# Routing two token blocks at a time, and all operand splits of an output phase on VectorE

## The chip, the cores and the metric

One core of one Trainium2 chip runs the whole program. The metric is the device time of one launch in microseconds (us). TensorE (PE) does the matrix products, VectorE (DVE), ScalarE (ACT) and GpSimd (POOL) the elementwise work; each engine runs its own queue of instructions in order, and SyncE (SP) issues most of the transfers. PEld is TensorE loading its weights, which goes on beside the products.

## What is computed

One decoder layer on 1024 tokens of width 1024: a norm and an input projection, two groups of causal attention heads, a norm for each group, an output projection, then a router and experts, and at the end a gated embedding and a norm. The change concerns the part from the output projection to the router:

```python
x = x + jnp.concatenate([o_sb, o_df], axis=-1) @ w_out
h2 = _rmsnorm(x, g_ffn).reshape(-1, D_MODEL)
group_logits = h2 @ w_router_group + b_router_group
g_idx = jnp.argmax(group_logits, axis=-1)
g_w = softmax(group_logits)[g_idx]
in_group = (h2 @ w_router_expert + b_router_expert)[group g_idx]
top_vals, top_idx = lax.top_k(in_group, 2)
top_w = softmax(top_vals) * g_w
for e in range(16):
    y = y + gates[:, e] * (silu(h2 @ w_gate[e]) * (h2 @ w_up[e])) @ w_down[e]
```

Each token goes to two of 16 experts. The kernel computes only these two: it numbers the tokens of each expert (their rank), keeps the lists of token numbers in `slots`, and later fetches the rows of an expert by an indirect transfer.

## The kernel before

The tokens are handled in eight blocks of 128. To keep accuracy every large operand is **split** into a rounded high part and a remainder: `split` (L53) rounds on ScalarE (L54) and subtracts on VectorE, or on the engine that is handed in (L55). A product then takes three matrix instructions, high by high, high by low, and low by high (L1162 to L1164).

Attention runs until about 590 us, its last part beside the first blocks of the output phase. The class `OutPhase` does for each block b: `normed(b)` (L1124), which loads the attention output, scales it (L1136, L1141) and splits it, on GpSimd for b of 2 and more (L1144); `proj_items(b)` (L1147), two halves of 24 products each with an addition on VectorE (L1166); `tail(b)` (L1201), which transposes the sum (L1194), splits the transposed tile from the accumulator memory (PSUM) (L1195), multiplies by the router's weights (L1210) and norms the block (L116); and `routes(b)`, the call of `route` (L1287), a chain of some 33 short instructions on VectorE. The chain takes the maximum of the group logits (L1298), marks the winner (`pick`, L1275), masks the other groups (L1308), picks the first and second expert (L1311 to L1316), adds both marks to `A` (L1325), has TensorE count ranks (L1327, L1328), builds two rows of marks (L1336), has TensorE put the token numbers in their places (L1343), and adds these to `slots` (L1345). `items(b)` (L1172) puts `normed(b + 1)` beside the second step of block b, and `tail(b - 1)` and `routes(b - 1)` among its later steps; the tail and the routing of the last block come after all of it.

Beside blocks 3 to 7 the weights of the first expert are loaded and split ahead: `moe.start` (L1667) splits three tiles on GpSimd, and at block 5 `moe.weights(1, nc.gpsimd)` two more (L1041). After the last routing `route_tail` (L1350) turns `slots` into lists of indices, while TensorE computes five blocks of the embedding's product (`ple_back`, L1465); then the rows of the first expert are fetched (L1507), transposed (L1516), and the experts' loop begins (L1681).

Outside the stretches marked as a manual schedule a planner orders each engine's queue before the program runs. It works with its own estimate of every instruction's length, and among instructions that it holds to be ready it takes the one that stands earlier in the program. On the chip the order is fixed: an engine stands before an instruction whose operands are late, even if a later one could go.

Of the kernel before, what the change touches and what calls it, by code (L numbers as in the profile page):

```python
# [25 lines left out]
CAP = 192  # L26
# [9 lines left out]
def bcast(ap, n):  # L36
    return bass.AP(tensor=ap.tensor, offset=ap.offset, ap=[[0, 128], [1, n]])
# [728 lines left out]
def run_items(*streams):  # L766

    tot = [sum(c for c, _ in s) or 1.0 for s in streams]
    pos = [0] * len(streams)
    done = [0.0] * len(streams)  # L770
    while True:
        live = [i for i in range(len(streams)) if pos[i] < len(streams[i])]
        if not live:
            return
        i = min(live, key=lambda x: (done[x] + 0.5 * streams[x][pos[x]][0]) / tot[x])
        c, f = streams[i][pos[i]]
        f()
        done[i] += c
        pos[i] += 1
# [36 lines left out]
def first_pair(k, P, pa, pp):  # L816
# [37 lines left out]
    def norm(b, parts=1):  # L854
        return normed(k, b, r[b], g, parts)
# [95 lines left out]
def phase_attention(k, moe, pq):  # L951
    nc, tc = k.nc, k.tc
# [12 lines left out]
    start = ExitStack()  # L965
# [101 lines left out]
class OutPhase:  # L1067
# [56 lines left out]
    def normed(self, b):  # L1124
        k, nc, wk = self.k, self.k.nc, self.wk
        if b % 2 == 0:
            self.scales(b // 2)
        rs = self.rs[b // 2]
        cols = lambda t: t.rearrange("p (c q) -> p c q", c=NC)
        raw = cols(self.oraw[b % 2])  # L1130
        nc.sync.dma_start(raw, k.oT_d[:, :, b * 128:(b + 1) * 128].rearrange("c p s -> p c s"))
        sc = lambda i: rs[:, b % 2, i:i + 1].to_broadcast([128, 128])
        bc = self.bank("t")
        nc.tensor.transpose(bc[:, 0:128], sc(0), k.ident)
        for c in range(4):
            nc.vector.scalar_tensor_tensor(raw[:, c, :], raw[:, c, :], self.gn[:, c:c + 1], bc[:, 0:128],  # L1136
                                           op0=OP.mult, op1=OP.mult)
        bc = self.bank("t")
        for i in range(4):
            nc.tensor.transpose(bc[:, i * 128:(i + 1) * 128], sc(1 + i), k.ident)  # L1140
        nc.vector.scalar_tensor_tensor(raw[:, 4:8, :], raw[:, 4:8, :], self.gn[:, 4:5],  # L1141
                                       bc.rearrange("p (c q) -> p c q", c=4), op0=OP.mult, op1=OP.mult)
        oh, ol = cols(self.onh[b % 2]), cols(self.onl[b % 2])
        split(nc, oh, ol, raw, nc.gpsimd if b > 1 else nc.vector)  # L1144
        self.O[b] = oh, ol

    def proj_items(self, b):  # L1147
# [74 lines left out]
        self.lg[b] = lg, r  # L1222

    def routes(self, b):
        route(self.k, b, *self.lg.pop(b))


def route_consts(k):
    nc = k.nc
    p = k.cp  # L1230
# [41 lines left out]
    nc.vector.memset(k.slots, 0.0)  # L1272


def pick(k, sc, m, n, wts):  # L1275

    nc, rt = k.nc, k.rt
    v = rt.tile([128, n], FT, name="pk_v", bufs=3)
    vm = rt.tile([128, 1], FT, name="pk_m", bufs=6)
    oh = rt.tile([128, n], FT, name="pk_o", bufs=6)  # L1280
# [3 lines left out]
    return oh, vm  # L1284


def route(k, b, lg, rstd):  # L1287
    nc, rt = k.nc, k.rt
    col = lambda nm: rt.tile([128, 1], FT, name=nm, bufs=2)
    L = rt.tile([128, 20], FT, name="L")  # L1290
    tp = k.bank("t")[:, 0:80]
    for x in range(2):
        nc.tensor.transpose(tp[:, 40 * x:40 * x + 40], lg[:, 128 * x:128 * x + 128], k.ident[0:40, 0:40])
    nc.vector.reduce_sum(L, tp.rearrange("p (x n) -> p n x", x=4), axis=AX)
    nc.vector.scalar_tensor_tensor(L, L, rstd, k.br, op0=OP.mult, op1=OP.add)
    G, E = L[:, 0:4], L[:, 4:20]
# [3 lines left out]
    eg = rt.tile([128, 4], FT, name="eg")  # L1300
    nc.scalar.activation(eg, G, AF.Exp, bias=ng, accum_out=sg)
    gw = col("gw")
    nc.vector.reciprocal(gw, sg)
    og, _ = pick(k, G, gm, 4, k.wt16[:, 12:16])
    pen = rt.tile([128, 4], FT, name="pen")
    nc.vector.tensor_scalar(pen, og, 1.0, 1e30, op0=OP.subtract, op1=OP.mult)
    Lm = rt.tile([128, 16], FT, name="Lm")
    nc.vector.tensor_tensor(Lm.rearrange("p (g e) -> p g e", g=4), E.rearrange("p (g e) -> p g e", g=4),  # L1308
                            pen[:, :, None].to_broadcast([128, 4, 4]), OP.add)
    m1, m2 = col("m1"), col("m2")  # L1310
    nc.vector.reduce_max(m1, Lm, axis=AX)  # L1311
    o1, _ = pick(k, Lm, m1, 16, k.wt16)
    L2 = rt.tile([128, 16], FT, name="L2")
    nc.vector.scalar_tensor_tensor(L2, o1, -3e30, Lm, op0=OP.mult, op1=OP.add)
    nc.vector.reduce_max(m2, L2, axis=AX)
    o2, _ = pick(k, L2, m2, 16, k.wt16)  # L1316
    d, e21, den = col("dd"), col("e21"), col("den")
    nc.vector.tensor_tensor(d, m2, m1, OP.subtract)
    nc.scalar.activation(e21, d, AF.Exp)
    nc.vector.tensor_scalar(den, e21, 1.0, None, op0=OP.add)  # L1320
    nc.vector.reciprocal(den, den)
    nc.vector.tensor_tensor(k.wts[:, 0, b:b + 1], den, gw, OP.mult)
    nc.vector.tensor_tensor(k.wts[:, 1, b:b + 1], k.wts[:, 0, b:b + 1], e21, OP.mult)
    A = rt.tile([128, 16], BF, name="A")
    nc.vector.tensor_tensor(A, o1, o2, OP.add)  # L1325
    rk = k.bank("sm")
    nc.tensor.matmul(rk[:, 0:16], k.tri, A, start=True, stop=False)  # L1327
    nc.tensor.matmul(rk[:, 0:16], k.onesb, k.acum, start=False, stop=True)  # L1328
    nc.vector.tensor_tensor(k.acum, k.acum, A, OP.add)
    put = []  # L1330
    for i, o in enumerate((o1, o2)):
        j16 = rt.tile([128, 16], FT, name="j16")
        r = k.rank[:, i, b:b + 1]
        nc.vector.scalar_tensor_tensor(j16, rk[:, 0:16], 1.0, o, op0=OP.mult, op1=OP.mult, accum_out=r)
        row = rt.tile([128, CAP], BF, name="row", bufs=2)
        nc.vector.tensor_scalar(row, k.ios, r, None, op0=OP.is_equal)  # L1336
        ids = rt.tile([128, 2, 16], BF, name="ids", bufs=2)
        nc.vector.tensor_tensor(ids, o[:, None, :].to_broadcast([128, 2, 16]),
                                k.tok[:, i, b, :, None].to_broadcast([128, 2, 16]), OP.mult)
        put.append((row, ids))  # L1340
    for rows, lo, n, x in (((0, 128), 0, 128, 32), ((0, 64), 128, 64, 64), ((64, 128), 128, 64, 64)):
        for i, (row, ids) in enumerate(put):
            nc.tensor.matmul(rk[rows[0]:rows[1], x:x + 32], row[:, lo:lo + n], ids.rearrange("p a e -> p (a e)"),  # L1343
                             start=(i == 0), stop=(i == 1))
    nc.vector.tensor_tensor(k.slots, k.slots, rk[:, 32:96].rearrange("p (s a e) -> p s a e", s=2, a=2), OP.add)  # L1345
    for i, o in enumerate((o1, o2)):
        nc.gpsimd.tensor_copy(k.chose[:, i, b, :], o)


def route_tail(k, rt):  # L1350
# [139 lines left out]
class Moe:  # L1490
# [513 lines left out]
```

## Time and profile before

| what | us |
|---|---|
| median of 3 runs (range) | 1231.78 (1230.64 to 1232.29) |
| the profiled execution, its own time | 1227.81 |
| its span, first to last instruction | 1226.0 |
| TensorE busy in it | 1145.5 (93%) |
| VectorE busy | 923.1 (75%) |
| ScalarE busy | 723.0 (59%) |
| GpSimd busy | 207.5 (17%) |
| mean granted TensorE clock | 0.979 of full speed |

Shares of the whole span mix stages with different limits. The stage of the change lies between about 500 and 702 us of the span, so that is where the rows of the prediction are read. An idle time of TensorE that stands in brackets behind a row of the timeline names what ended it.

### The profile page before, as it was taken

The numbers are of one execution on the slowest core, as the hardware profiler recorded it, in microseconds if no ns is written. First come the engines' busy times: TensorE is split into PE (matmuls) and PEld (weight loads), VectorE is DVE, ScalarE is ACT, GpSimd is POOL, SyncE is SP. The second block draws the span as 40 slices with busy tenths as digits, with TensorE's granted clock in tenths as the row PEclk, the third lists the DMA queues.
The fourth block names the chain that finished last, engine by engine and source line by source line (L and its number), as shares of the span: only waits on it lengthen the run. The fifth ranks groups of instructions, "written<-read, shape, count | busy, mean of one in ns | idle before, by whom it ended". The sixth has DMA issues, their size and how long they took to land. (4 is left out here: it accounts for less than half of the span.)

```text
span 1226.0 us, 22814 instructions
## 1 busy us (share of the span) xinstructions
PE 1145.5 (93%) x8181; PEld 826.5 (67%) x8181; DVE 923.1 (75%) x2144; ACT 723.0 (59%) x1408; POOL 207.5 (17%) x298
## 2 busy tenths in 40 slices
PE   5999999999999999889789899999999999997996
PEld 4766656665666666646444498898998989883443
DVE  7677786766766767769888777777888878765875
ACT  6476766766756576735332365666777767663432
POOL 0133333333200000002331101111112212110000
PEclk9999999999999999879899999999999999999999
DMA  6212021120222121532674878998998999937611
GB/s 208 67 30 74 30 69 32 44 60 27 57 61 65 40 65 53 171 90 102 217 234 148 298 250 262 282 352 265 316 313 283 337 280 325 304 125 298 250 71 52
DMA packets 211756, 202.54 MB, mean 165 GB/s; under 512 B 12697, under 2 KB 182681, under 8 KB 211642
## 3 DMA queue, kind: packets, MB, share of 16 engines
q1 hardware_dynamic: 205688, 180.22, 46.9%
q0 software_dynamic: 5808, 20.58, 4.5%
q8 instruction: 65, 1.06, 0.3%
q14 instruction: 49, 0.40, 0.1%
q10 hardware_dynamic: 146, 0.27, 0.1%
HBM read 163.03 MB, written 29.62 MB: 157 GB/s over the span
## 5 line engine op out<-in xcount | busy, mean ns | idle before, releaser
L228 PE MATMUL mm<-hT,whi 128*128 128x512 f32 (+1 forms) x416 | 210.9, 508 | 2.6 <-DVE rs_v L66 1.4
L229 PE MATMUL mm<-hT,whi 128*128 128x512 bf16 (+1 forms) x416 | 157.0, 377 | 4.1 <-DVE hT L184 4.1
L230 PE MATMUL mm<-hT,wlo 128*128 128x512 bf16 (+1 forms) x416 | 155.7, 374 | 0.0
L1611 PE MATMUL gu<-xh,mhiu 128*128 128x128 f32 (+4 forms) x512 | 155.1, 314 | 0.0
L1611 PE MATMUL gu<-xh,mhig 128*128 128x128 f32 (+4 forms) x512 | 153.9, 308 | 0.0
L1613 PE MATMUL gu<-xbl,mhig 128*128 128x128 bf16 (+4 forms) x512 | 124.6, 243 | 2.6 <-DVE xbl L1524 2.6
L1613 PE MATMUL gu<-xbl,mhiu 128*128 128x128 bf16 (+4 forms) x512 | 124.4, 243 | 0.0
L1614 PE MATMUL gu<-xh,mblg 128*128 128x128 bf16 (+4 forms) x512 | 119.6, 234 | 0.0
L1614 PE MATMUL gu<-xh,mblu 128*128 128x128 bf16 (+4 forms) x512 | 119.3, 233 | 0.0
L55 DVE TENSOR_TENSOR mdl<-mrawd,mdh 128x1024 bf16<-128x1024 f32 x63 | 77.0, 1222 | 44.6 <-ACT mdh L54 39.9
L54 ACT ACTIVATE wth<-tp 128x512 fp32r<-128x512 f32 (+2 forms) x168 | 70.2, 446 | 63.0 <-PE tp L378 41.0
L55 DVE TENSOR_TENSOR wtl<-tp,wth 128x512 fp32r<-128x512 f32 (+2 forms) x168 | 79.2, 493 | 36.7 <-ACT wth L54 35.3
L409 POOL TENSOR_TENSOR row<-row,keep 128x127 f32<-128x127 f32 (+3 forms) x64 | 77.9, 1218 | 143.5 <-DVE keep L408 88.4
L228 PEld LDWEIGHTS mm<-hT,whi 128*128 128x128 f32 x416 | 80.2, 193 | 30.9 <-ACT hT L183 2.0
L55 DVE TENSOR_TENSOR mblg<-mrawg,mhig 128x1024 bf16<-128x1024 f32 x62 | 75.8, 1223 | 29.8 <-ACT mhig L54 29.7
L54 ACT ACTIVATE mdh<-mrawd 128x1024 fp32r<-128x1024 f32 x64 | 67.6, 1056 | 51.8 <-PE ya L1643 47.6
L1611 PEld LDWEIGHTS gu<-xh,mhig 128*128 128x128 f32 x512 | 97.6, 191 | 0.7 <-ACT xh L1523 0.3
L229 PEld LDWEIGHTS <-whi 128*128 128x128 bf16 x416 | 40.7, 98 | 85.0 <-issue 78.6
L1611 PEld LDWEIGHTS gu<-xh,mhiu 128*128 128x128 f32 x512 | 96.7, 189 | 0.0
L408 DVE TENSOR_TENSOR_SCAN keep<-keep,zx 128x128 f32<-128x128 f32 (+3 forms) x64 | 85.4, 1346 | 14.1 <-ACT keep L404 13.4
L46 POOL DMA_INDIRECT y_d<-yo,put x27 | 44.6, 1651 | 290.0 <-ACT yo L1661 185.8
L54 ACT ACTIVATE mhig<-mrawg 128x1024 fp32r<-128x1024 f32 x64 | 67.4, 1053 | 19.2 <-PE gu L1614 11.9
(348 smaller groups left out, 3346.6 us busy)
## 6 DMA issues: line engine op xcount, KB each, us to landing
mrawg<-in_w_expert_gate_dram SPq DMA_DIRECT2D x64, 512.0 KB, 5.8
mrawu<-in_w_expert_up_dram SPq DMA_DIRECT2D x64, 512.0 KB, 6.4
mrawd<-in_w_expert_down_dram SPq DMA_DIRECT2D x64, 512.0 KB, 4.3
wraw<-in_w_in_dram SPq DMA_DIRECT2D x24, 512.0 KB, 3.9
yg<-y_d SPq DMA_DIRECT2D x16, 512.0 KB, 5.7
xt<-in_x_dram SPq DMA_DIRECT2D x8, 512.0 KB, 6.6
oT_d<-ot SPq DMA_DIRECT2D x32, 128.0 KB, 2.1
wraw<-in_w_out_dram SPq DMA_DIRECT2D x8, 512.0 KB, 3.6
```

What stands on the lines that cost most here:

```text
L46: i = k.nc.gpsimd.indirect_dma_start(out=out, out_offset=bass.IndirectOffsetOnAxis(ap=idx, axis=0), in_=src, in_offset=None)
L54: nc.scalar.activation(hi, src, AF.Copy)
L55: (eng or nc.vector).tensor_tensor(lo, src, hi.bitcast(FT), OP.subtract)
L228: nc.tensor.matmul(ps, hi[:, c, :], hT[:, c % 4, :], start=(c == 0), stop=False)
L229: nc.tensor.matmul(ps, wv[:, c, :], k.hT[half][2][:, c, o:o + n], start=False, stop=False)
L230: nc.tensor.matmul(ps, lo[:, c, :], hv[:, c % 4, :], start=False, stop=(c == NC - 1))
L408: nc.vector.tensor_tensor_scan(a, a, k.zeros.to_broadcast([128, n]), 1.0, op0=OP.mult, op1=OP.add)
L409: nc.gpsimd.tensor_tensor(beta[:, :n - 1], beta[:, :n - 1], keep[:, 1:n], OP.mult)
L1611: nc.tensor.matmul(ps[:, x], hi[:, c], xh[:, c], start=(c == 0), stop=False)
L1613: nc.tensor.matmul(ps[:, x], hv[:, c], xl[:, c], start=False, stop=False)
L1614: nc.tensor.matmul(ps[:, x], bl[:, c], xv[:, c], start=False, stop=(c == NC - 1))
```

## The change

The routing is cut in two. `logits` makes the 20 logits of one block and leaves them in half of a shared tile `k.L`; it runs where `route` ran. `route` now runs after each odd block only, on both blocks at once: its small tiles get a dimension of two. As the maximum that `pick` compares with is no longer one value per partition, its first instruction (compare and multiply) becomes two. The ranks of the second block are counted with one more product, which adds the first block's `A`. The four rows of marks are built one after the other, their twelve products go to separate places of one PSUM bank, and one reduction adds them up before `slots` is updated. The weights of the two experts (`k.wts`) and the copy to `chose` on GpSimd come last, once for both blocks.

All five weight tiles split ahead, and the attention output of blocks 2 to 7, are split on VectorE. GpSimd keeps the copies to `chose`, the memsets and the indirect transfers.

```diff
-            moe.weights(1, nc.gpsimd)
+            moe.weights(1)
...
-        split(nc, oh, ol, raw, nc.gpsimd if b > 1 else nc.vector)
+        split(nc, oh, ol, raw)
...
     def routes(self, b):
-        route(self.k, b, *self.lg.pop(b))
+
+        logits(self.k, b, *self.lg.pop(b))
+        if b % 2:
+            route(self.k, b - 1)
...
-    nc.vector.scalar_tensor_tensor(v, sc, m, wts, op0=OP.is_equal, op1=OP.mult)
+    nc.vector.tensor_tensor(v, sc, over(m), OP.is_equal)
+    nc.vector.tensor_tensor(v, v, wts[:, None, :].to_broadcast([128, 2, n]), OP.mult)
     nc.vector.reduce_max(vm, v, axis=AX)
-    nc.vector.tensor_scalar(oh, v, vm, None, op0=OP.is_equal)
...
+    nc.vector.tensor_tensor(oh, v, over(vm), OP.is_equal)
...
+    A = one("A", 16, BF)
+    nc.vector.tensor_tensor(A, O[:, 0], O[:, 1], OP.add)
+    rk = k.bank("sm")
+    for y in range(2):
+        r = rk[:, 16 * y:16 * y + 16]
+        nc.tensor.matmul(r, k.tri, A[:, y], start=True, stop=False)
+        if y:
+            nc.tensor.matmul(r, k.onesb, A[:, 0], start=False, stop=False)
+        nc.tensor.matmul(r, k.onesb, k.acum, start=False, stop=True)
+    nc.vector.tensor_tensor(k.j16, rk[:, 0:32].rearrange("p (y e) -> p y e", y=2)[:, None].to_broadcast([128, 2, 2, 16]),
+                            O, OP.mult)
+    nc.vector.reduce_sum(k.rank[:, :, two], k.j16, axis=AX)
+    for i in range(2):
+        nc.vector.tensor_tensor(k.ids[:, i], O[:, i, :, None, :].to_broadcast([128, 2, 2, 16]),
+                                k.tok[:, i, two, :, None].to_broadcast([128, 2, 2, 16]), OP.mult)
+    for i in range(2):
+        for y in range(2):
+            row = rt.tile([128, CAP], BF, name="row", bufs=2)
+            nc.vector.tensor_scalar(row, k.ios, k.rank[:, i, b + y:b + y + 1], None, op0=OP.is_equal)
+            ids = k.ids[:, i, y].rearrange("p a e -> p (a e)")
+            for rows, lo, n, x in (((0, 128), 0, 128, 32), ((0, 64), 128, 64, 64), ((64, 128), 128, 64, 64)):
+                x += 64 * (2 * i + y)
+                nc.tensor.matmul(rk[rows[0]:rows[1], x:x + 32], row[:, lo:lo + n], ids, start=True, stop=True)
+    new = k.j16.rearrange("p i y e -> p (i y e)")
+    nc.vector.reduce_sum(new, rk[:, 32:288].rearrange("p (z n) -> p n z", z=4), axis=AX)
+    nc.vector.tensor_tensor(k.slots, k.slots, new.rearrange("p (s a e) -> p s a e", s=2, a=2), OP.add)
+    for y in range(2):
+        nc.vector.tensor_tensor(k.acum, k.acum, A[:, y], OP.add)
...
     def start(self):
         self.wp = self.pool("mw", 2)
-        self.weights(0, self.k.nc.gpsimd)
-        self.weights_down(0, self.k.nc.gpsimd)
+        self.weights(0)
+        self.weights_down(0)
```

## Rows read from the trace of the kernel before

**Rows 1.** Busy time of each engine in a stretch of 20 us: stretch, its length, then PE, PEld, DVE, ACT and POOL busy with their instructions, granted TensorE clock, share of the DMA engines, GB/s.

```profile
580.00:600.00 20.00, 17.16 (x103) 10.31 (x101) 18.03 (x66) 9.12 (x18) 9.12 (x8) 1.00 0.80 270
```

**Rows 2.** Timeline of TensorE: start, length, instruction, and in brackets the idle time before it and what ended it.

```profile
577.36 0.66 PE L378 MATMUL tp<-ident,row 128*128 128x128 f32 x4 [0.79 <-DVE wtl L55]
...
603.91 1.07 PE L1210 MATMUL dsm<-od,wr 128*40 128x256 f32 x4 [6.74 <-DVE od L55]
...
619.32 0.19 PE L1343 MATMUL dsm<-ids,row 128*128 128x32 bf16 x1 [1.28 <-DVE row L1336]
...
633.00 0.17 PE L1327 MATMUL dsm<-A,tri 128*128 128x16 bf16 x1 [2.10 <-DVE A L1325]
...
653.80 0.17 PE L1327 MATMUL dsm<-A,tri 128*128 128x16 bf16 x1 [2.06 <-DVE A L1325]
...
663.95 0.18 PE L1327 MATMUL dsm<-A,tri 128*128 128x16 bf16 x1 [0.28 <-DVE A L1325]
```

**Rows 3.** The same columns as in rows 1, in stretches of 4 us around two of those idle times.

```profile
604.00:608.00 4.00, 4.00 (x15) 2.35 (x16) 0.56 (x3) 0.38 (x1) 0.00 (x0) 0.50 1.03 312
608.00:612.00 4.00, 4.00 (x16) 1.68 (x15) 3.58 (x16) 2.28 (x4) 1.05 (x1) 0.87 0.11 31
...
632.00:636.00 4.00, 3.00 (x15) 1.55 (x14) 2.75 (x26) 0.20 (x1) 0.20 (x1) 0.62 1.06 275
```

**Rows 4.** The splits on GpSimd: all of them by the tile that they write (lengths in ns, lowest/median/highest, then first and last start).

```profile
L55 POOL TENSOR_TENSOR od<-od,od x6: 2358/2388/2878, 554.4 to 650.6; 128x1024 bf16<-128x1024 f32 x6
L55 POOL TENSOR_TENSOR mblg<-mrawg,mhig x2: 2371/2380/2388, 591.0 to 615.7; 128x1024 bf16<-128x1024 f32 x2
L55 POOL TENSOR_TENSOR mblu<-mrawu,mhiu x2: 2378/2380/2381, 593.7 to 622.4; 128x1024 bf16<-128x1024 f32 x2
L55 POOL TENSOR_TENSOR mdl<-mrawd,mdh x1: 2336/2336/2336, 598.7 to 598.7; 128x1024 bf16<-128x1024 f32 x1
```

**Rows 5.** Timeline of VectorE: instructions that began beside a split on GpSimd, one of the same kind with no such split beside it (590.96), and the two splits of a transposed block that TensorE waited for (603.17).

```profile
573.29 2.35 DVE L80 TENSOR_SCALAR rs_y<-rs_i 128x1 int32<-128x1 int32 x2
...
590.96 0.17 DVE L71 TENSOR_TENSOR rs_t<-rs_t,rs_v 128x10 f32<-128x10 f32 x1
591.07 2.31 DVE L75 SCALAR_TENSOR_TENSOR rs_t<-rs_y,rs_v 128x1 f32<-128x1 f32 x1
...
594.99 1.13 DVE L84 TENSOR_SCALAR rs_t<-rs_t 128x1 f32<-128x1 f32 x2
...
596.38 2.34 DVE L71 TENSOR_TENSOR rs_t<-rs_y 128x10 f32<-128x10 f32 x1
...
598.75 2.26 DVE L71 TENSOR_TENSOR rs_t<-rs_t,rs_v 128x10 f32<-128x10 f32 x1
...
603.17 1.28 DVE L55 TENSOR_TENSOR od<-dt,od 128x512 fp32r<-128x512 f32 x2
...
615.79 2.35 DVE L1323 TENSOR_TENSOR wts<-wts,e 128x1 f32<-128x1 f32 x1
...
622.64 2.14 DVE L71 TENSOR_TENSOR rs_y<-rs_y,rs_t 128x1 f32<-128x1 f32 x1
...
650.62 2.35 DVE L1281 SCALAR_TENSOR_TENSOR pk_v<-L,m,wt 128x16 f32<-128x16 f32 x1
```

**Rows 6.** A split of the same shape on VectorE, two of them as a group of the stretch from 540 to 690 us: busy time, mean ns of one, idle before.

```profile
L55 DVE TENSOR_TENSOR pll<-mrawd,plh 128x1024 bf16<-128x1024 f32 x2 | 2.4, 1214 | 0.0
```

**Rows 7.** Timeline of VectorE: the routing of block 5 (its second instruction, the rows of marks, the last), the addition of a projection within it, and a reduction of 256 elements elsewhere.

```profile
659.27 0.24 DVE L1295 SCALAR_TENSOR_TENSOR L<-L,rs_y,br 128x20 f32<-128x20 f32 x1
...
662.58 0.68 DVE L1166 TENSOR_TENSOR od<-mm,od 128x512 f32<-128x512 f32 x1
...
664.49 0.45 DVE L1336 TENSOR_SCALAR row<-ios,rank 128x192 bf16<-128x192 bf16 x2
...
665.40 0.22 DVE L1345 TENSOR_TENSOR slots<-slots,dsm 128x64 f32<-128x64 f32 x1
...
692.40 0.41 DVE L1377 TENSOR_REDUCE cn_place<-cn_m 128x16 f32<-128x256 f32 x1
```

**Rows 8.** The end of the phase, from the timelines of three engines: the last instruction of the last projection, the last routing's second and last instruction, the second fetch, the last product of the embedding, and the first transpose for the experts.

```profile
677.10 0.39 PE L1164 MATMUL mm<-woh,od 128*128 128x512 bf16 x1
...
697.09 0.39 PE L1476 MATMUL pq<-plh,pTl 128*128 128x512 bf16 x1
699.18 0.71 PE L1516 MATMUL mt<-ident,xr 64*128 64x64 f32 x8 [1.71 <-DMA xr<-h_d,idx]
...
683.74 0.23 DVE L1295 SCALAR_TENSOR_TENSOR L<-L,rs_y,br 128x20 f32<-128x20 f32 x1
...
690.42 0.22 DVE L1345 TENSOR_TENSOR slots<-slots,dsm 128x64 f32<-128x64 f32 x1 [0.67 <-PE dsm L1343]
...
693.61 0.91 POOL L1507 DMA_INDIRECT xr<-h_d,idx  x1 [0.30 <-PE pq L1476]
```

**Rows 9.** What TensorE waited for from 702 us to the end, the largest: total us, times, longest.

```profile
PE pq L1459 <- issue: 4.9, 1, 4.9
```

**Rows 10.** Timeline of ScalarE, the high parts of two of the weight tiles; and from the page's costliest groups the experts' own splits on VectorE (busy, mean ns, idle before and what ended most of it).

```profile
592.58 1.06 ACT L54 ACTIVATE mhiu<-mrawu 128x1024 fp32r<-128x1024 f32 x1 [1.69 <-DMA mrawu<-in_w_expert_up_dram]
...
621.24 1.06 ACT L54 ACTIVATE mhiu<-mrawu 128x1024 fp32r<-128x1024 f32 x1
...
L55 DVE TENSOR_TENSOR mblg<-mrawg,mhig 128x1024 bf16<-128x1024 f32 x62 | 75.8, 1223 | 29.8 <-ACT mhig L54 29.7
```

More of the change, by code (lines that the diff above doesn't have):

```diff
@@ L1272, in route_consts, with pick, logits @@
     nc.vector.memset(k.slots, 0.0)
-def pick(k, sc, m, n, wts):
+def pick(k, sc, m, n, wts, oh):
     nc, rt = k.nc, k.rt
-    v = rt.tile([128, n], FT, name="pk_v", bufs=3)
-    vm = rt.tile([128, 1], FT, name="pk_m", bufs=6)
-    oh = rt.tile([128, n], FT, name="pk_o", bufs=6)
-    nc.vector.scalar_tensor_tensor(v, sc, m, wts, op0=OP.is_equal, op1=OP.mult)
-    nc.vector.reduce_max(vm, v, axis=AX)
-    nc.vector.tensor_scalar(oh, v, vm, None, op0=OP.is_equal)
[L1284 to L1290, printed above, removed]
+    over = lambda x: x[:, :, None].to_broadcast([128, 2, n])
+    v = rt.tile([128, 2, n], FT, name="pk_v", bufs=2)
+    vm = rt.tile([128, 2], FT, name="pk_m", bufs=3)
+    nc.vector.tensor_tensor(v, sc, over(m), OP.is_equal)
+    nc.vector.tensor_tensor(v, v, wts[:, None, :].to_broadcast([128, 2, n]), OP.mult)
+    nc.vector.reduce_max(vm, v, axis=AX)
+    nc.vector.tensor_tensor(oh, v, over(vm), OP.is_equal)
+def logits(k, b, lg, rstd):
+    nc = k.nc
     tp = k.bank("t")[:, 0:80]
@@ L1293, in route @@
         nc.tensor.transpose(tp[:, 40 * x:40 * x + 40], lg[:, 128 * x:128 * x + 128], k.ident[0:40, 0:40])
+    L = k.L[:, b % 2, :]
     nc.vector.reduce_sum(L, tp.rearrange("p (x n) -> p n x", x=4), axis=AX)
     nc.vector.scalar_tensor_tensor(L, L, rstd, k.br, op0=OP.mult, op1=OP.add)
-    G, E = L[:, 0:4], L[:, 4:20]
+def route(k, b):
+    nc, rt = k.nc, k.rt
+    two = slice(b, b + 2)
+    col = lambda nm: rt.tile([128, 2], FT, name=nm, bufs=1)
+    one = lambda nm, n, t=FT: rt.tile([128, 2, n], t, name=nm, bufs=1)
+    G, E = k.L[:, :, 0:4], k.L[:, :, 4:20]
     gm, ng, sg = col("gm"), col("ng"), col("sg")
@@ L1299, in route @@
     nc.vector.tensor_scalar(ng, gm, -1.0, None, op0=OP.mult)
[L1300 to L1309, printed above, removed]
+    eg = one("eg", 4)
@@ L1310, in route @@
+    for y in range(2):
+        nc.scalar.activation(eg[:, y], G[:, y], AF.Exp, bias=ng[:, y:y + 1], accum_out=sg[:, y:y + 1])
+    og = one("og", 4)
+    pick(k, G, gm, 4, k.wt16[:, 12:16], og)
+    nc.vector.tensor_scalar(og, og, 1.0, 1e30, op0=OP.subtract, op1=OP.mult)
+    Lm = one("Lm", 16)
+    nc.vector.tensor_tensor(Lm.rearrange("p y (g e) -> p y g e", g=4), E.rearrange("p y (g e) -> p y g e", g=4),
+                            og[:, :, :, None].to_broadcast([128, 2, 4, 4]), OP.add)
     m1, m2 = col("m1"), col("m2")
+    O = rt.tile([128, 2, 2, 16], FT, name="pk_o", bufs=2)
@@ L1311, in route @@
     nc.vector.reduce_max(m1, Lm, axis=AX)
[L1312 to L1317, printed above, removed]
+    pick(k, Lm, m1, 16, k.wt16, O[:, 0])
+    nc.vector.scalar_tensor_tensor(Lm, O[:, 0], -3e30, Lm, op0=OP.mult, op1=OP.add)
+    nc.vector.reduce_max(m2, Lm, axis=AX)
@@ new lines, in route @@
+    pick(k, Lm, m2, 16, k.wt16, O[:, 1])
+    A = one("A", 16, BF)
[9 more added lines that the diff above has]
+                            O, OP.mult)
@@ L1318, in route @@
+    new = k.j16.rearrange("p i y e -> p (i y e)")
+    nc.vector.reduce_sum(new, rk[:, 32:288].rearrange("p (z n) -> p n z", z=4), axis=AX)
+    nc.vector.tensor_tensor(k.slots, k.slots, new.rearrange("p (s a e) -> p s a e", s=2, a=2), OP.add)
+    for y in range(2):
+        nc.vector.tensor_tensor(k.acum, k.acum, A[:, y], OP.add)
+    d, e21, gw = col("dd"), col("e21"), col("gw")
     nc.vector.tensor_tensor(d, m2, m1, OP.subtract)
     nc.scalar.activation(e21, d, AF.Exp)
-    nc.vector.tensor_scalar(den, e21, 1.0, None, op0=OP.add)
@@ L1321, in route @@
[L1321 to L1347, printed above, removed]
+    nc.vector.reciprocal(gw, sg)
@@ L1350, in route_tail @@
+    nc.vector.tensor_scalar(d, e21, 1.0, None, op0=OP.add)
+    nc.vector.reciprocal(d, d)
+    nc.vector.tensor_tensor(k.wts[:, 0, two], d, gw, OP.mult)
+    nc.vector.tensor_tensor(k.wts[:, 1, two], k.wts[:, 0, two], e21, OP.mult)
+    nc.gpsimd.tensor_copy(k.chose[:, :, two, :], O)
 def route_tail(k, rt):
```

4 lines of the change are left out of this document (added).

## The prediction

> **What bounds the kernel now.** I read the busy time by stretches first. In the stage of the change TensorE is the engine to follow, and VectorE comes next: from 580 to 600 us TensorE is busy for 17.16 of 20 us and VectorE for 18.03 [rows 1]. So I went to TensorE's timeline and looked for the idle times that something ended [rows 2]. From 560 to 677 us those over half a microsecond are 0.79, 6.74, 1.28, 2.10 and 2.06 us, and each was ended by VectorE. Two of them are followed by a lower clock. TensorE stands at half its clock, the lower of its two levels, in the 4 us after the wait of 6.74, and the next 4 us average 0.87. That loses 4.00 x 0.50 + 4.00 x 0.13 = 2.5 us. After the wait of 2.10 us, 3.00 busy us at 0.62 lose 1.1 us [rows 3]. The sum is 13.0 us idle and 3.6 us of clock, 16.6 us. This is all that the change can win before the phase's end.
>
> Why was VectorE late? GpSimd runs eleven splits of about 2.38 us each [rows 4]. Beside most of them one short instruction of VectorE, of a kind that takes 0.17 us, takes 2.1 to 2.35 us [rows 5]. Both its operands lie in SBUF; a pair of instructions that began within a split took 1.13. Between 591.07 and 603.17 four such stretches add 2.31 + 1.13 + 2.34 + 2.26 less some 0.8 of own length, 7.2 us; at 603.17 VectorE at last begins the split that TensorE has been waiting for since 597.2 [rows 2, 5]. The stretches at 615.79 and 650.62 lie in the chains whose ends TensorE waits for at 619.32 and 653.80, those at 573.29 and 622.64 shortly ahead of the waits at 577.36 and 633.00. The waits on the marks' sum A that had no such stretch ahead of them come to 0.28 us in all [rows 2, 5]. That is the argument for the whole forecast.
>
> **The change part by part.** *The splits.* Eleven leave GpSimd. The eight long rows add up to 17.2 us for ten instructions, whose own length would be 1.7, so the stretches cost VectorE 15.5 us [rows 5]. Eleven splits of 1.21 us come onto it, 13.4 us [rows 6]. VectorE's load falls by about 2 us, and no split lasts longer than 1.22 where it lasted 2.38.
>
> The Trainium skill ("Perfetto Trace Analysis", section "Optimizing Scalar/DVE Operations") speaks against this part: with a saturated VectorE, work may be moved from it, even to GpSimd. It adds that the two engines share a port, so that this might not help. By the first half alone VectorE would get 13.4 us more in a stage where it is 90% busy; by the rows it gets 2 us less.
>
> *The routing's load.* From L1295 to the end of L1345 block 5 takes 665.62 - 659.27 = 6.35 us, less 0.68 for an addition within it, 5.7 us for 32 instructions, 0.18 each [rows 7]. Two blocks take some 66 instructions, 12 us. By the diff the pair takes 42. At 0.18 each and 0.4 more for wider tiles that is 8.0 us, so VectorE is relieved of 4 us for each pair, 16 us in the phase. None of this is on TensorE's path by itself. What counts is that the chain no longer runs at blocks 0, 2, 4, 6.
>
> *The wait of 6.74.* Without the stretches VectorE has 12.1 - 7.2 = 4.9 us of its own work from 591.07 to the awaited split. In its place three splits now come ahead of that split in program order (two weight tiles and the attention output), 3.6 us, or four with the third weight tile, 4.9 us. The routing of blocks 0 and 1 ends just before and is longer than the single one by 1.8 us (below); against that stand some 1.5 us of norm steps of later blocks, which the planner can leave until later. So the awaited split begins at 591.1 + 4.9 + 3.6 + 0.3 = 599.9 instead of 603.2. With less loss at the low clock (between the 1.1 us after a wait of 2.10 and the 2.5 after 6.74) I take 4.0 us won. The bounds are 1 us (the fourth split ahead, and the norm steps not put off) and 8.5 us (the awaited split goes ahead of them all, and the full clock stays).
>
> *The waits of 1.28, 2.10, 2.06 and 0.79*, with 1.1 us of clock, hold 7.3 us. The chain of block 2, which held the 1.28, is gone from that place. The chains of blocks 3 and 4 become one of the pair 2 and 3 and, later, one of the pair 4 and 5. I leave 0.5 us of waiting for each of these two pairs and 0.3 for the rest, and take 6.0 us won (bounds 2 and 7.3).
>
> *The end of the phase.* The last routing now does two blocks. From L1295 to L1345 it took 6.68 us [rows 8]. Behind it come the index lists, the fetch at 693.61, and the first transpose at 699.18, for which TensorE had already waited 1.71 us with nothing left to do after 697.09 + 0.39 [rows 8]. So every microsecond that this chain grows is paid in full. It grows by one instruction in each of three picks, at 0.23 us each, 0.7 us (block 5 took 665.40 - 659.27 = 6.13 us from L1295 to L1345, less 0.68 for the addition, over the 24 dependent steps that I count in the code); by two more rows of marks at 0.45 for two, 0.45; by one step for the ranks, 0.23; and by the reduction of 256 elements, 0.41 [rows 7]. That is 1.8 us, with bounds of 0.9 (rows and reduction half hidden beside the products) and 3.0 (wide tiles that take half as long again). No row shows these operations on two blocks; the nearest are those of the single chain, and so I take the middle. The longer wait may bring 0.5 us more at the low clock (0 to 1). Together 2.3 us lost.
>
> The Trainium skill (same page and section) says of bubbles on other engines that breaking instructions up may let work finish sooner. At this place the change does the opposite, and by that rule it loses; the rows give the 1.8 us above.
>
> *No cost.* The copies to `chose` stay on GpSimd, half as many. The products of the routing are 17 for each pair in place of 16, all short. No transfer is added; SP's queue is unchanged but for what its issues wait for. What is won here is not lost later: from 702 us on TensorE's largest single wait is 4.9 us near the end, and none of its waits is on a weight transfer [rows 9].
>
> **The sum.** 4.0 + 6.0 - 2.3 = 7.7 us. The profiled execution took 1227.81 us (span 1226.0), so one like it would take 1220.1. The median of the runs is 4.0 us above it, and the forecast for the median is 1231.78 - 7.7 = 1224.1, say 1224 us.
>
> **The rivals.** *Everything comes back:* the planner's order suits the chip once nothing stretches, all 16.6 us are won, and the end costs 0.9. Then 1216. For it: the small waits where no split ran beside [rows 2]. Against it: VectorE still has three splits ahead of the awaited one. *VectorE as full as before:* its queue fills with splits as it was filled with stretches, and only the chain of block 2 and its neighbours gain, some 4 us, less 2.3 at the end: 1230. For it: it is 90% busy there [rows 1]. Against it: the sum of its load, 2 + 16 us less. This is also what the skill's rule on a saturated VectorE would give.
>
> *Slower: VectorE stands before a load.* Its queue is in order, and a weight split needs ScalarE's high part, which needs the transfer. If the planner holds the transfer to be early, the split stands at the head of VectorE's queue, behind it the norm steps, the projection's additions and the transposed blocks' splits, and TensorE waits for all of these. ScalarE did stand 1.69 us before such a tile at 592.58, the same tile of the next weights was ready for the rounding only at 621.24, and in the experts' loop VectorE stands 29.8 us in 62 cases before ScalarE's high parts, 0.5 us each [rows 10]. Five tiles at 0.5 us do no harm. The sign turns when VectorE stands for over 7.7 us in all, which the first tile pair at 592 and the second at 615 to 622 could make up (3 + 6 us, and 3 us at the low clock): 7.7 - 12 gives 4 us slower, 1236. Against it: the tiles' splits on GpSimd followed ScalarE at once in the timeline, so the planner's order was late enough there.
>
> *It doesn't do what it says:* the stretches have another cause and stay. Then the waits stay, VectorE gets 13.4 us on top, and the result is that of the third rival; I count it there.
>
> **How the numbers follow.** Forecast (1219 to 1228) 0.55, all comes back 0.13, as full as before 0.16, slower 0.16. A measurement of this kernel can tell about 0.2%, 2.5 us, from no change, so faster means under 1229.3. The first two cases and a little of the third, whose 1230 lies on that edge, give 0.70 faster; most of the third 0.13 same; the rest 0.17 slower. The range from 1215 to 1233 takes in the bounds of the sum (7.3 + 8.5 - 0.9 = 14.9 won, 2 + 1 - 4 = 1 lost) and the first three cases, and leaves out the fourth and little else.
>
> **What would show it.** Right: no VectorE instruction of one to ten elements a partition over 1 us between 550 and 690 us; the wait of 6.74 at 2 to 4; no wait on A over 1 us; the transpose for the experts at some 691 us, with about 3.5 us of waiting ahead of it. Wrong: VectorE's waits on ScalarE for weight tiles of over 2 us; TensorE's wait on the awaited split still 6; the end's chain over 10 us; or a TensorE order that has changed before 540 us.

## The result

| | us |
|---|---|
| median before (range of 4 runs) | 1231.21 (1228.72 to 1232.29) |
| median after (range of 4 runs) | 1215.72 (1215.23 to 1216.34) |
| ratio, 95% interval | 0.9883, 0.987 to 0.9896 |
| profiled execution after, its own time; its span | 1215.36; 1213.6 |
| TensorE, VectorE, GpSimd busy in it | 1139.2, 907.6, 177.9 |

The change won 15.5 us by the medians, where 7.7 were forecast. Between the two profiled executions it is 12.4 us, since the one of before lies 3.4 us under its median. That gap is not seen in a trace, but on record the executions of the kernel before tended to take longer the lower their mean granted clock was: of 36 beside the later runs, the six at 0.979 to 0.981 took 1227.1 to 1229.1 us, as the profiled one did at 0.979, and the six at 0.974 and 0.975 took 1231.0 to 1234.0.

The stage of the change in the profile after, by stretches of 20 us, columns as in [rows 1]:

```profile
580.00:600.00 20.00, 19.84 (x115) 11.69 (x118) 18.43 (x79) 9.87 (x20) 0.49 (x3) 1.00 0.91 301
600.00:620.00 20.00, 19.86 (x105) 10.86 (x104) 18.43 (x49) 9.77 (x17) 0.00 (x0) 1.00 0.88 284
620.00:640.00 20.00, 19.86 (x113) 10.80 (x113) 17.52 (x69) 6.02 (x10) 0.27 (x1) 1.00 0.63 212
640.00:660.00 20.00, 19.66 (x111) 10.60 (x112) 12.36 (x60) 5.19 (x14) 0.27 (x1) 1.00 0.45 161
```

TensorE is busy throughout, at the full clock. VectorE is as busy from 580 to 600 us as it was in [rows 1], 18.43 against 18.03, and nobody waits for it. The answer to [rows 2], all that TensorE waited for from 555 to 660 us after the change (total, times, longest):

```profile
PE zx L1353 <- DVE rs_v L66: 0.2, 1, 0.2
PE mm L1164 <- issue: 0.2, 1, 0.2
PE dsm L1336 <- DVE A L1332: 0.2, 1, 0.2
```

The answer to [rows 5], VectorE around the split that TensorE used to wait for, and TensorE and ScalarE in the same stretch (start, length, instruction, idle time before it):

```profile
591.09 0.21 DVE L75 SCALAR_TENSOR_TENSOR rs_t<-rs_y,rs_v 128x1 f32<-128x1 f32 x1
...
593.13 1.22 DVE L55 TENSOR_TENSOR mblu<-mrawu,mhiu 128x1024 bf16<-128x1024 f32 x1
...
596.12 1.22 DVE L55 TENSOR_TENSOR mdl<-mrawd,mdh 128x1024 bf16<-128x1024 f32 x1
597.26 1.22 DVE L55 TENSOR_TENSOR od<-od,od 128x1024 bf16<-128x1024 f32 x1
598.39 1.28 DVE L55 TENSOR_TENSOR od<-dt,od 128x512 fp32r<-128x512 f32 x2
599.59 0.21 DVE L75 SCALAR_TENSOR_TENSOR rs_t<-rs_y,rs_v 128x1 f32<-128x1 f32 x1
```

```profile
597.32 0.39 PE L1164 MATMUL mm<-woh,od 128*128 128x512 bf16 x1
...
599.42 0.83 PE L1210 MATMUL dsm<-od,wr 128*40 128x256 f32 x4
```

```profile
594.55 1.06 ACT L54 ACTIVATE mdh<-mrawd 128x1024 fp32r<-128x1024 f32 x1 [3.04 <-DMA mrawd<-in_w_expert_down_dram]
```

No short instruction is stretched any more. Every split lasts 1.22 us. ScalarE waited 3.04 us for a weight tile, but VectorE reached that tile's split only when it was ready. The router's products at 599.42 have no idle time before them.

The answers to [rows 8], the end of the phase after the change, on TensorE, VectorE and GpSimd:

```profile
660.20 0.39 PE L1164 MATMUL mm<-woh,od 128*128 128x512 bf16 x1
...
686.24 1.12 PE L1536 MATMUL mt<-ident,xr 64*128 64x64 f32 x8 [5.32 <-DMA xr<-h_d,idx]
```

```profile
666.94 0.24 DVE L1302 SCALAR_TENSOR_TENSOR L<-L,rs_y,br 128x20 f32<-128x20 f32 x1
...
675.54 0.23 DVE L1356 TENSOR_TENSOR slots<-slots,rspare 128x64 f32<-128x64 f32 x1
675.68 0.42 DVE L1395 TENSOR_TENSOR cn_m<-cn_key 128x256 f32<-128x256 f32 x1
...
677.80 0.16 DVE L1391 TENSOR_SCALAR idx<-cn_i 128x2 int32<-128x2 int32 x1
```

```profile
679.87 0.91 POOL L1527 DMA_INDIRECT xr<-h_d,idx  x1 [0.30 <-PE pq L1496]
```

I count the stage from the phase's first transposition (L1134, at 526.50 before and 526.88 after) to the last product of the last projection. It took 677.10 - 526.50 = 150.60 us before and 133.32 after: 17.3 us won. From there to the first transposition for the experts it took 22.08 us before [rows 8] and takes 26.04 after: 4.0 lost. From that transposition to the end of the span it is 526.9 and 527.3: 0.5 lost. With 0.4 us lost ahead of the stage this is the 12.4 us between the two spans. The gain is more than forecast, and so is the loss at the end.

### The profile page after: what moved, and what is told of

Same layout as the page of the kernel before. It is cut to its first block, busy times and chain, and to the rows that moved or that the text cites. A ratio compares the mean times of both kernels' runs of the same rounds, so it can differ in the third digit from the quotient of the medians.

```text
span 1213.6 us, 22567 instructions
## 1 busy us (share of the span) xinstructions
PE 1139.2 (94%) x8076; PEld 826.2 (68%) x8185; DVE 907.6 (75%) x2043; ACT 722.7 (60%) x1404; POOL 177.9 (15%) x275
## 5 line engine op out<-in xcount | busy, mean ns | idle before, releaser
L229 PE MATMUL mm<-hT,whi 128*128 128x512 bf16 (+1 forms) x378 | 142.3, 376 | 4.3 <-DVE hT L184 4.3
L55 DVE TENSOR_TENSOR mdl<-mrawd,mdh 128x1024 bf16<-128x1024 f32 x64 | 78.2, 1222 | 44.6 <-ACT mdh L54 40.6
L55 DVE TENSOR_TENSOR mblg<-mrawg,mhig 128x1024 bf16<-128x1024 f32 x64 | 78.3, 1223 | 29.8 <-ACT mhig L54 28.5
```

The source lines that it names most:

```text
L229: nc.tensor.matmul(ps, wv[:, c, :], k.hT[half][2][:, c, o:o + n], start=False, stop=False)
```

## The experiments

Three theories stood at the start. Theory 1: GpSimd's long subtractions held up VectorE, and ending that is the gain. Theory 2: the routing in pairs relieves VectorE, and that is the gain. Theory 3: the queues are ordered anew when the splits change engines, and the new order is the gain. For the end of the phase: the chain of two blocks is longer, and the list of slots stands later in VectorE's queue. The table gives what each run measured; stage and end are counted as above, in each run's own trace. They come from one profiled execution of each kernel, and executions of one kernel differ by up to 7 us, so differences of 1 us between them show little by themselves.

| kernel | median (before beside it) | ratio, 95% interval | stage | end |
|---|---|---|---|---|
| before | | | 150.60 | 22.08 |
| after | 1215.72 (1231.21) | 0.987 to 0.9896 | 133.32 | 26.04 |
| 1 splits only | 1214.59 (1230.63) | 0.9848 to 0.9892 | 133.60 | 23.84 |
| 2 pairs only | 1228.25 (1230.63) | 0.997 to 1.0 | 142.97 | 25.70 |
| 3 idle subtractions | 1226.57 (1230.63) | 0.9949 to 0.9979 | 143.73 | 26.57 |
| 4 last two single, list first | 1213.19 (1230.63) | 0.9834 to 0.9877 | 132.72 | 22.74 |
| 5 weight tiles only | 1220.03 (1229.18) | 0.9905 to 0.9933 | 140.85 | 22.03 |
| 6 attention output only | 1221.91 (1229.18) | 0.9927 to 0.9959 | 144.46 | 23.12 |
| 7 idle writes | 1216.46 (1229.18) | 0.9879 to 0.9909 | 132.35 | 26.69 |
| 8 list first | 1215.14 (1229.18) | 0.9863 to 0.9901 | 132.32 | 25.14 |
| 9 after, again | 1216.13 (1229.54) | 0.9864 to 0.9904 | 133.63 | 26.30 |
| 10 splits only, list first | 1213.41 (1229.54) | 0.9846 to 0.9888 | 133.51 | 24.20 |
| 11 as 4, again | 1212.58 (1229.54) | 0.9835 to 0.988 | 132.63 | 23.22 |

**Run 1: splits only.** Against before:

```diff
-            moe.weights(1, nc.gpsimd)
+            moe.weights(1)
...
-        split(nc, oh, ol, raw, nc.gpsimd if b > 1 else nc.vector)
+        split(nc, oh, ol, raw)
...
-        self.weights(0, self.k.nc.gpsimd)
-        self.weights_down(0, self.k.nc.gpsimd)
+        self.weights(0)
+        self.weights_down(0)
```

> The kernel before with all splits of the phase on VectorE, and its routing block by block as before. Theory 1 (GpSimd's long subtractions held up VectorE's short instructions, and the awaited split was slow on GpSimd; the splits are what won): the four waits of TensorE in 600 to 660 us go, and the end of the phase stays as short as before, so about 1213 to 1216 us, no slower than the changed kernel. Theory 2 (the routing's fewer instructions on VectorE are what won; VectorE with the splits and the old routing is as full as before): 1225 to 1231 us, with new waits of TensorE on VectorE between 560 and 660 us.

It took 1214.59 us. The old routing, block by block, costs the stage nothing once the splits are on VectorE: 133.60 us, 133.32 with the pairs. The largest waits of TensorE from 555 to 672 us in this run:

```profile
PE dt L1293 <- ACT od L1212: 0.6, 2, 0.5
PE mm L1164 <- DVE od L55: 0.5, 1, 0.5
PE pq L1474 <- ACT spare L1477: 0.5, 1, 0.5
```

Theory 2 falls as the cause of the gain.

**Run 2: pairs only.** Against after, the diff of run 1 backwards.

> The changed kernel with the splits put back on GpSimd, so that only the routing in pairs is left of the change. Theory 1 (the splits won): short VectorE instructions of 2.1 to 2.4 us are back, the awaited split is back at about 2.4 us on GpSimd, and the longer chain at the end of the phase is paid without a gain: 1231 to 1236 us. Theory 2 (the routing won): 1217 to 1222 us, with few waits of TensorE in 560 to 660 us.

It took 1228.25 us. VectorE's instructions of over 1 us that are short elsewhere, and one of 0.15 us (613.52) that began beside the same GpSimd split as the next:

```profile
572.96 2.40 DVE L66 TENSOR_SCALAR rs_v<-ss 128x10 f32<-128x10 f32 x1
...
592.43 2.33 DVE L71 TENSOR_TENSOR rs_t<-rs_t,rs_v 128x10 f32<-128x10 f32 x1
...
594.80 2.31 DVE L84 TENSOR_SCALAR rs_t<-rs_t 128x10 f32<-128x10 f32 x1
...
613.52 0.15 DVE L90 TENSOR_SCALAR rs_i<-rs_t 128x1 f32<-128x1 f32 x1
...
613.96 1.80 DVE L71 TENSOR_TENSOR rs_y<-rs_y,rs_i 128x1 f32<-128x1 f32 x1
...
644.57 1.81 DVE L71 TENSOR_TENSOR rs_y<-rs_y,rs_i 128x1 f32<-128x1 f32 x1
```

Theory 1 expected no gain, and that was too little, though theory 2's 1217 to 1222 us was missed by more. With the splits on GpSimd the pairs do shorten the stage, by 7.6 us in the trace: five rows are stretched where there were eight long ones [rows 5]. The end takes back 3.6, and of the whole kernel's time 2.4 us are won, with an interval that reaches no gain. So in these traces the relief counts only as long as GpSimd gets in the way.

**Run 3: idle subtractions.** Against after; the call stands behind each split that the change moved, eleven in the trace (the expectation says thirteen). The pieces are read from the split's own operands and written to a tile that nobody reads.

```diff
+def idle(k, src, hi):
+    for x in range(0, D, 256):
+        k.nc.gpsimd.tensor_tensor(k.junk, src[:, x:x + 256], hi.bitcast(FT)[:, x:x + 256], OP.subtract)
```

> The changed kernel, in which GpSimd does the subtractions of the thirteen moved splits once more (in four pieces of 256 columns each) into a tile that nobody reads; the instructions of TensorE, VectorE and ScalarE stand in the same order as in the changed kernel. Theory 1 (two engines at SBUF get in each other's way): short VectorE instructions beside GpSimd's subtractions last 1 to 2 us again, and some of the 17 us come back: 1220 to 1230 us. Theory 3 (the won time comes from the order in which the instructions are now queued, with the products of the projection between the transposes and the router, and from the awaited split being shorter; GpSimd's work beside VectorE does no harm by itself): 1215 to 1217 us, even where short instructions are stretched.

It took 1226.57 us, 10.9 more than the changed kernel's 1215.72, though no engine's computation needs these subtractions, and TensorE, VectorE and ScalarE run the same instructions in the same order in both traces. SyncE's queue did wait for them twice before it loaded an attention output, 2.4 us in all, but no engine then waited for such a load. TensorE's largest waits from 526 to 672 us are all on VectorE:

```profile
PE dsm L1218 <- DVE od L61: 2.9, 2, 1.6
PE dt L1146 <- DVE L L1310: 2.1, 1, 2.1
PE dsm L1345 <- DVE A L1341: 1.9, 1, 1.9
```

The costliest groups of VectorE from 550 to 665 us (busy, mean ns), first of after, then of this run:

```profile
L1166 DVE TENSOR_TENSOR od<-mm,od 128x512 f32<-128x512 f32 x14 | 9.6, 685 | 0.5 <-PE mm L1164 0.4
L116 DVE SCALAR_TENSOR_TENSOR od<-od,rs_y,od 128x1024 f32<-128x1024 f32 x7 | 9.0, 1285 | 0.1
L55 DVE TENSOR_TENSOR od<-dt,od 128x512 fp32r<-128x512 f32 x12 | 8.0, 686 | 4.6 <-ACT od L54 4.5
L55 DVE TENSOR_TENSOR od<-od,od 128x1024 bf16<-128x1024 f32 x6 | 7.3, 1219 | 0.0
```

```profile
L122 DVE SCALAR_TENSOR_TENSOR od<-od,rs_y,od 128x1024 f32<-128x1024 f32 x7 | 10.7, 1523 | 0.1
L61 DVE TENSOR_TENSOR od<-od,od 128x1024 bf16<-128x1024 f32 x6 | 9.3, 1546 | 0.0
L1174 DVE TENSOR_TENSOR od<-mm,od 128x512 f32<-128x512 f32 x12 | 8.2, 681 | 0.4 <-PE mm L1172 0.3
L61 DVE TENSOR_TENSOR od<-dt,od 128x512 fp32r<-128x512 f32 x10 | 6.6, 680 | 0.4 <-ACT od L60 0.4
...
L61 DVE TENSOR_TENSOR pll<-mrawd,plh 128x1024 bf16<-128x1024 f32 x2 | 3.4, 1746 | 0.0
```

Instructions with both tensors in SBUF lengthen: 1285 to 1523 ns, 1219 to 1546, and the 1214 of [rows 6] to 1746. Those that take one tensor from PSUM (`mm`, `dt`) stay as short, 685 and 686 ns after, 681 and 680 here. Theory 1 holds. Its expectation for the short instructions was too high: beside these shorter pieces they lasted 0.5 to 0.8 us, not 1 to 2. The 10.9 us are not the contention's share in the kernel before: here VectorE has its own splits as well, and GpSimd is busy for 44 us with the pieces.

**Run 7: idle writes.** The counterpart of run 3, in the same places:

```diff
+def idle(k, src, hi):
+    k.nc.gpsimd.tensor_tensor(k.junk[:, 0:1], src[:, 0:1], hi.bitcast(FT)[:, 0:1], OP.subtract)
+    for _ in range(10):
+        k.nc.gpsimd.memset(k.junk.bitcast(FT), 0.0)
```

> The changed kernel, in which GpSimd, at each of the thirteen places, reads one column and then fills an unread tile ten times with zeros, about 2.1 us of writes, in place of the four subtractions of the run with idle subtractions; the instructions of TensorE, VectorE and ScalarE stand in the same order again. If it is GpSimd's reads of SBUF that shut out VectorE: 1215 to 1217 us, and VectorE's subtractions of 1024 columns stay at 1.22 us. If any work of GpSimd at SBUF shuts it out: 1222 to 1227 us, and they last 1.5 us as beside the idle subtractions.

It took 1216.46 us. GpSimd wrote for 22.6 us in the phase, and VectorE's groups are as after the change; they and GpSimd's own:

```profile
L123 DVE SCALAR_TENSOR_TENSOR od<-od,rs_y,od 128x1024 f32<-128x1024 f32 x7 | 9.0, 1284 | 0.1
...
L62 DVE TENSOR_TENSOR od<-od,od 128x1024 bf16<-128x1024 f32 x6 | 7.3, 1217 | 0.0
```

```profile
L57 POOL MEMSET junk<- 128x128 f32 x110 | 22.6, 205 | 6.3
```

It is GpSimd's reads of SBUF that hold up VectorE's instructions with two tensors from SBUF. The two runs differ in one thing more, as GpSimd holds the split's operands longer in run 3; the lengthened instructions above do not depend on that. The Trainium skill ("SBUF — State Buffer", section "Who interferes with whom") says the same: such an instruction contends with a GpSimd instruction that reads SBUF and not with one that only writes, and one with at most one SBUF input does not contend, unless it runs in a mode that uses two ports. Runs 3 and 7 agree with the first two. The exception matters here, though no trace tells an instruction's mode: beside GpSimd's subtractions, TENSOR_SCALAR instructions with one tensor in and ten elements were held up too (572.96 and 594.80 in run 2, 2.40 and 2.31 us), while those of one element kept 0.14 to 0.21 us in all these traces (613.52 in run 2).

**Run 5: weight tiles only.** Against before, the first and third parts of run 1's diff.

> The kernel before, in which only the five weight tiles are split on VectorE; the attention output of blocks 2 to 7 stays on GpSimd, the routing is as before, and TensorE's queue stands as before up to the transposes behind the 6.74 us wait. Theory 1 (what GpSimd does beside VectorE, and what is queued on GpSimd ahead of the awaited split, makes the waits): the awaited split no longer stands behind three weight tiles, the 6.74 us wait falls to 2 to 4 us, and with fewer stretched instructions the time is 1220 to 1226 us. Theory 3 (the order of TensorE's queue makes the difference): the wait stays over 5 us, and the time is 1227 to 1231 us.

It took 1220.03 us. Of the wait of 6.74 only 0.40 is left, before the second half, though TensorE still has only two groups of products between the transposes and the router; TensorE, VectorE and GpSimd at that place:

```profile
598.72 0.83 PE L1210 MATMUL dsm<-od,wr 128*40 128x256 f32 x4
```

```profile
597.35 0.68 DVE L1166 TENSOR_TENSOR od<-mm,od 128x512 f32<-128x512 f32 x1
597.95 0.68 DVE L55 TENSOR_TENSOR od<-dt,od 128x512 fp32r<-128x512 f32 x1
598.55 1.23 DVE L84 TENSOR_SCALAR rs_t<-rs_t 128x1 f32<-128x1 f32 x2
```

```profile
597.35 2.40 POOL L55 TENSOR_TENSOR od<-od,od 128x1024 bf16<-128x1024 f32 x1 [7.07 <-ACT od L54]
```

One split of GpSimd's is left here. Beside it run two instructions that read PSUM, 0.68 us each as ever, and one pair of short ones that is stretched to 1.23. Theory 3 expected a wait of over 5 us at this place and falls for it; theory 1 expected 2 to 4.

**Run 6: attention output only.** Against before, the second part of run 1's diff.

> The kernel before, in which only the attention output of blocks 2 to 7 is split on VectorE and the five weight tiles stay on GpSimd; TensorE's queue is reordered as in the run with all splits on VectorE, up to the second pair of blocks. Theory 1 (GpSimd's subtractions beside VectorE cost time): short VectorE instructions of over 2 us are left beside the five weight tiles, and the time lies between, 1217 to 1224 us. Theory 3 (the new order of the queues is enough): 1213 to 1216 us.

It took 1221.91 us, and three waits are left or new:

```profile
PE dsm L1327 <- DVE A L1325: 3.9, 2, 3.3
PE dt L1134 <- DVE slots L1345: 3.7, 1, 3.7
PE z L1343 <- DVE row L1336: 1.5, 1, 1.5
```

TensorE's instructions stand here as in run 1 up to 597.0 us. The wait of 1.5 lies in that stretch, ended at 594.99, where run 1 has none; ahead of it a VectorE instruction of 16 elements (L1329, 592.22) lasted 2.19 us beside a split on GpSimd. The stage takes 144.46 us, not 133.60. The order alone does not do it. The stage's gains of runs 5 and 6, 9.8 and 6.1 us, add up to 15.9 of run 1's 17.0; by the medians they won 9.2 and 7.3 of 16.0.

**Runs 4 and 8: the end of the phase.** Run 8, against after:

```diff
-    nc.vector.tensor_scalar(k.idx0, i0, S - 1, None, op0=OP.bitwise_and)
+    first = nc.vector.tensor_scalar(k.idx0, i0, S - 1, None, op0=OP.bitwise_and)
...
+    with k.tc.issue_after(first.ins):
+        nc.vector.scalar_tensor_tensor(key, cnt[:, 0:16], 16.0, k.io, op0=OP.mult, op1=OP.subtract)
```

> The changed kernel, with the list of slots for the first expert computed ahead of the instructions of the ranking and nothing else. Theory of the end (the second fetch is issued 1.1 us late because of the order of VectorE's queue): it is issued 1.0 us sooner after the last projection, and the time is 1214.5 to 1215.0 us. Rival (the transfer ends no sooner, since the queues of the transfers are full then): the time is 1215.5 to 1216.0 us.

The second fetch came 18.85 us after the last projection, 0.82 sooner than after the change (19.67), and the first transposition 0.90 sooner. The time, 1215.14 us (1212.61 to 1217.18), can't be told from the changed kernel's: that the place of the list delays the fetch is shown, what this costs the kernel is not.

Run 4 has this too, and routes blocks 6 and 7 by themselves (`route1` is the single routing in halves of the pair's tiles):

```diff
-        if b % 2:
+        if b > 5:
+            route1(self.k, b)
+        elif b % 2:
             route(self.k, b - 1)
```

> The changed kernel, with the last two blocks (6 and 7) routed one by one, block 6 early, and with the list of slots computed ahead of the instructions of the ranking. Theory of the end (the chain of the last routing is 1.9 us longer in pairs, and the second fetch is issued another 1.1 us late because of the order of VectorE's queue): the first transpose of the experts comes 2.5 to 3.5 us sooner after the last projection, and the time is 1212.0 to 1213.5 us. Rival (the fetched rows or the first expert's weights are late in any case, or the low clock of the stage eats it): 1215 to 1216 us.

It took 1213.19 us. Its second fetch and first transposition:

```profile
677.05 0.91 POOL L1599 DMA_INDIRECT xr<-h_d,idx  x1 [0.30 <-issue]
```

```profile
683.57 0.71 PE L1608 MATMUL mt<-ident,xr 64*128 64x64 f32 x8 [2.80 <-DMA xr<-h_d,idx]
```

The fetch is issued 16.22 us after the last projection (660.83), where it took 16.51 before [rows 8] and 19.67 after. The end takes 22.74 us in place of 26.04, 3.3 less, as expected.

**Runs 9 to 11: side by side.** After once more, run 1 with the list first, and run 4 once more.

> The changed kernel once more, unaltered, so that the next two are compared with it on the same chip: 1214.5 to 1217 us.

> All splits on VectorE, routing block by block as before, and the list of slots ahead of the ranking. If the routing in pairs is worth nothing once the splits are on VectorE (theory 1), the shorter end makes it 1 to 3 us faster than the changed kernel beside it. If the pairs keep VectorE from falling behind, it is no faster than that kernel.

> Pairs for blocks 0 to 5, blocks 6 and 7 one by one, and the list first, the same as in the fourth run, beside the other two: 2 to 3 us faster than the changed kernel, and within 1 us of the run with single routing throughout.

Run 9's executions lie between 1215.56 and 1217.23 us, run 10's between 1212.16 and 1214.70, run 11's between 1209.09 and 1214.77. Both variants beat the changed kernel, by 2.7 and 3.5 us of the medians (run 11 expected 2 to 3). Against each other they can't be told apart. Both differ from run 9 in the list as well as in the routing, so this is not the price of the pairs alone. Like with like, the stage took 133.60 us in run 1 and 133.51 in run 10 without the pairs, and 132.32 to 133.63 with them (after, runs 8 and 9), and the end is shorter without: 23.84 in run 1 against 26.04 after, and 24.20 in run 10 against 25.14 in run 8, where both have the list first. So once the splits had moved, the routing in pairs bought nothing that stands out of the noise, and lengthened the end by 0.9 to 2.2 us.

## Why the prediction was right, and where it was off

**The argument held, its size did not.** TensorE was waiting for VectorE, and VectorE for GpSimd's subtractions. Without them no short instruction is stretched and no wait of over 0.2 us is left from 555 to 660 us. Runs 3 and 7 show the mechanism, run 1 that the splits alone carry it. How much of the gain is the end of the stretches, and how much that a split takes 1.22 us and not 2.38, no run separates. But the gain was twice the forecast. The 15.5 us by the medians are more than the 14.9 of the sum's own best case, and 1215.72 lies only 0.7 us inside the stated range. That it lies inside was luck: the stage won 7.3 us more than forecast, and the end lost 2.2 more. The reading of [rows 5] needs one correction too. Two of its long rows (573.29 and 594.99) are of instructions with one tensor in, so not all of the stretched ones had two operands in SBUF.

**The wait of 6.74 was the term most mis-sized:** 4.0 us forecast, all 6.74 and the 2.5 of clock won. The step that failed is the start of the awaited split. It was put at 599.9, and it began at 598.39, although all four splits went ahead of it, which I had counted towards the lower bound. From 591.09 on VectorE did only 598.39 - 591.09 - 4 x 1.22 = 2.4 us of other work, where I had counted 4.9: the norm steps went behind the awaited split, from 599.59 on, and so gave back more than the 1.5 us that I had allowed them. TensorE was not waiting at 597.2 either: nearly three more groups of products now stand between the transposes and the router, so it came for the split at 599.42. Had the order stayed, it would have come at 597.32 + 0.39 = 597.71, and waited until the first of the two halves was done, at some 598.39 + 0.68 = 599.1. This 1.4 us is an estimate from the rows above, and the only part of this gain that I can put down to the new order. In run 5, under the old order, the split began at 597.95, in time as well.

**The waits of 1.28, 2.10, 2.06 and 0.79** were put at 6.0 of 7.3 us and gave all of it: where I had left 0.5 for each pair, there is 0.16 at one pair and no wait at the other. Together the stage won 17.3 us, not 10.0; the idle and clock that I had counted as the most it could win were 16.6.

**The routing's relief** was said to count because the chain no longer runs at blocks 0, 2, 4 and 6. Runs 1 and 2 show that this holds only beside GpSimd's splits, where the relief is worth 7.6 us of the stage; without them it is worth 0.3.

**The end** was put at 2.3 us, and cost 4.0 up to the first transposition and 0.5 behind it. The chain itself was right: from L1302 to L1356 it takes 675.54 - 666.94 = 8.60 us, 1.9 more than the 6.68 of [rows 8], with 1.8 forecast. The Trainium skill's rule on breaking instructions up ("Perfetto Trace Analysis", section "Optimizing Scalar/DVE Operations"), which spoke against this step, agrees. The 0.5 for the clock fits the loss behind the transposition by luck. In the first 7.8 us from there (686.24 to 694) the granted clock was 0.50 and 0.59, where it had been 0.77 and 0.80 before (699.18 to 707). Counted as in the prediction, with 3.25 and 4.00 busy us after and 3.07 and 4.00 before, that loses 3.3 and 1.5 us, so 1.8 more, and where 1.3 of it came back is not shown. Two terms were missing. The list of slots now stands behind the ranking's first instructions in VectorE's queue (L1391 at 677.80, behind L1395 at 675.68), and the second fetch comes 679.87 - 675.54 = 4.33 us after the last addition to `slots` began, 693.61 - 690.42 = 3.19 before, so 1.1 us later; run 8 gets 0.8 of this back. And the rows landed 686.24 - 679.87 = 6.37 us after the second fetch, 5.57 before [rows 8]. This 0.8 has no experiment. Run 1, whose end is 1.8 us longer than before without any pairs, shows that the pairs are not the cause of either: the fetch there comes 4.06 us after that addition began, and the rows 6.54 after the fetch.

**The rivals.** "Everything comes back" named 1216 us and had the stage right; its end of 0.9 was not. What I held against it, the splits ahead of the awaited one, cost the wait nothing. VectorE was as full as before and it did no harm, so the third rival fell, and the Trainium skill's rule that would also give it (the same page and section) would have misled here in its first half: taking work back from GpSimd onto a VectorE that is 90% busy made the kernel faster. Its remark that the shared port may undo such a move is the half that decides. The fourth rival needed VectorE to stand before a late weight tile; one tile was 3.04 us late for ScalarE, and VectorE did not stand.

## What to carry to other kernels

Read busy shares together with the lengths of short instructions: a 0.17 us instruction that lasts 2.3 beside a GpSimd subtraction means that the work which was moved off VectorE is still paid there, and the engine's 90% is partly such waiting. Here it paid to move back work that reads two SBUF tensors and that VectorE does in half the time; work that only writes could have stayed on GpSimd. Batching a chain of small steps shortened the middle of the phase only while VectorE was late, and lost where the chain's last instance was on the path, so the last blocks are better routed singly.

## What the runs showed of the hardware

In run 3 both sides lengthen. VectorE's subtraction of 1024 columns went from 1.22 to 1.55 us in the mean. GpSimd's 44 pieces of 256 columns are of two kinds: thirty took 0.73 to 0.75 us, also beside VectorE instructions that read PSUM, and thirteen took 1.58 to 1.82, each beside a VectorE instruction with two SBUF tensors of 1024 columns (one took 0.95).

An instruction's operands decide, and being short is no protection. Beside GpSimd's subtractions of 1024 columns, instructions with two SBUF tensors of one element lasted up to 2.37 us (L71 in run 6), and those with one tensor of 10 or 16 elements up to 2.40 (L66 in run 2; L1283 took 1.60 and 1.66 in runs 5 and 6). Those with one tensor of one element kept 0.14 to 0.21 us, reductions of 16 elements 0.15 to 0.16, and additions and subtractions of 512 columns that read PSUM 0.68 to 0.69.

The fetch of the first rows landed 5.57 and 5.54 us after its issue in the kernel before and in run 5, where the last load of the embedding gate's weights (`fraw`) had been issued 5.8 us ahead of it, and 6.2 to 7.7 us after it in the eleven other traces, where that load was 1.5 to 4.6 us ahead. This was seen and not tested.
